# A decoder layer in split fp32: the first stage begins with another order of loads and norm weights, and three plain feature tiles instead of two

## The chip, the cores and the metric

The kernel runs on one core of one Trainium2 chip. Five engines work side by side, each through its own queue in order: TensorE (PE; its weight loads are shown apart as PEld), VectorE (DVE), ScalarE (ACT), GpSimd (POOL) and SyncE (SP, which here only issues DMAs). They meet through semaphores. The metric is the device time of one execution in microseconds. The kernel before took 1367.01 us (median of three runs, 1365.49 to 1369.76).

## What is computed

One decoder layer on 512 tokens of width 1024, in fp32. Every sub-layer stands between an RMSNorm before and one after. Only the first lines matter for the change:

```python
def rmsnorm(x, w):
    y = xf * lax.rsqrt(jnp.mean(xf * xf, axis=-1, keepdims=True) + EPS)
    return (y * w.astype(jnp.float32)).astype(x.dtype)
def swiglu(x, w_gu, w_down):                     # w_gu: 1024 x 5632, w_down: 2816 x 1024
    g, u = jnp.split(x @ w_gu, 2, axis=-1)
    return (jax.nn.silu(g) * u) @ w_down
h = h + 0.5 * rmsnorm(swiglu(rmsnorm(h, ffn1_pre_w), ffn1_w_gu, ffn1_w_down), ffn1_post_w)
h = h + rmsnorm(token_mixing(rmsnorm(h, mix_pre_w), ...), mix_post_w)
h = h + 0.5 * rmsnorm(swiglu(rmsnorm(h, ffn2_pre_w), ffn2_w_gu, ffn2_w_down), ffn2_post_w)
```

The token mixing (a gated linear recurrence, a dilated attention and a memory attention, gated and projected) lies in the middle and is not edited.

## The kernel before

**Number form.** Every fp32 operand is split into a rounded part (`hi`, made by ACT, line 161) and the rest (`lo`, made by DVE, line 158). A product is three matmuls in the fast fp32r form: hi with hi, hi with lo, lo with hi (`mm3`, lines 341 to 343). Tiles are called `xhi`/`xlo` for the normed, transposed input, `w` for both halves of a weight tile, `st` for a weight tile as loaded (a ring of 4, 512 KB each), `s` for general slots, `ps` and `px` for PSUM banks (5 and 3).

**Two ways to make a feature tile.** A feature tile is 128 columns of the gate weights with the 128 matching columns of the up weights, over all 512 tokens. In the plain way (`gu_plain`, line 444) it takes 2 weight columns x 8 slices of the inner dimension x 3 passes x 2 token halves = 96 matmuls of 256 columns. In the other way (`gu` and `pair`, lines 435 and 366) the two columns are one 2x2 block product made of 7 smaller products, 7 x 4 x 3 = 84 matmuls of 256 columns (`product`, lines 361 to 363). That way needs sums of weight blocks (`sum` tiles, a ring of 5; two per tile are made by DMAs that POOL issues and that add `sh` or `st` onto a loaded block, line 303) and sums of input blocks (`t1` to `t4`), which exist only when all four token tiles are normed.

**The opening.** Of the 22 feature tiles of the first stage, the first two (`PLAN`, line 49) are plain, so that TensorE can begin with the first 256 tokens. `first` (line 1022) loads the token tiles 0 and 1 (two halves of 256 KB each) and the norm weights, spread to all 128 partitions by two DMAs of 256 KB (`bcast_gain`, line 164). Each token tile then goes through `normed` (line 184): two squares with a running sum on ACT (line 174), the variance on DVE (line 180), the power -1/2 on POOL (line 181), two products with the norm weights on DVE (line 190), eight transposes on TensorE (line 352). `prenorm` splits the result (`split`, line 160) and keeps a raw copy for the block sums (line 208). In this part `strict` is set: DMAs, ACT's and DVE's main instructions keep the order of the program. Later a list scheduler orders each engine by estimated times, and `spawn`, `tick` and `need` decide when a task's next piece is written.

**After it** come 20 feature tiles in the 7-product way, in chunks of 2, 4, 4, 4, 4, 4 features; the down projections of a chunk stand between the feature tiles of the next. Then the mixing and a second feed-forward stage of the same form, which starts from token tiles that come out of the stage before it.

Of the kernel before, what the change touches and what calls it, by code (L numbers as in the profile page):

```python
# [17 lines left out]
P = 128  # L18
# [28 lines left out]
LAT = dict(comb=1.0, mem0=0.5, mem1=8.0, mem2=1.5, hg=1.5, hgx=6.0, hg1=6.0, hg2=11.0, hg3=6.0, hg4=6.0, dil0=4.0, dil1=17.0, dil2=5.0,  # L47
           dil3=3.0, norm=8.0, mnorm=5.0, mload=10.0, start=0.1, step=2.0, keep=2.0)
PLAN = dict(early1=2, plain1=2, early2=2, plain2=2)
HALVES = (slice(0, 512), slice(512, 1024))  # L50


class Layer:
# [3 lines left out]
    def __init__(self, ctx, tc):  # L57
# [30 lines left out]

        self.strict = False


# [72 lines left out]
    def bcast_gain(self, w):  # L164
# [4 lines left out]
        return g  # L169

    def square(self, src, hf, step):

        s = self.small.tile([P, 1], F32, tag=f"ss{hf}", bufs=8, name=f"ss{hf}_{self.uid()}")
        self.pin(self.nc.scalar.activation(self.slot(src.shape), src, AF.Square, scale=1.0 / (32.0 * step), accum_out=s))
        return s
# [7 lines left out]

    def normed(self, src, gain, lat, bank):

        r = self.rstd([self.square(src[hf], hf, 1.0) for hf in range(2)], 1.0)
        us = []
        for hf in range(2):
            u = self.slot()
            self.pin(self.nc.vector.scalar_tensor_tensor(out=u, in0=src[hf], scalar=r, in1=gain[hf], op0=ALU.mult, op1=ALU.mult))  # L190
            us.append(u)
        yield lat
        for hf, u in enumerate(us):
            pt = bank((P, 4, P))
            for k in range(4):
                self.transpose(pt[:, k, :], u[:, k * P:(k + 1) * P])
            yield pt

    def prenorm(self, src, gain, t, lat, raw):
# [6 lines left out]
        def keep(hf):  # L206
            raw[t, hf] = self.slot((P, 4, P))
            nc.scalar.copy(raw[t, hf], pts[hf])

        wait = self.strict and t < 2  # L210
        for x in self.normed(src, gain, lat, self.psum if self.strict and t == 1 else self.paux):
            if isinstance(x, float):
                yield x
                continue
            hf = len(pts)
            pts.append(x)
            self.split(self.xhi[hf][:, :, ts], self.xlo[hf][:, :, ts], x)
            if not wait and (t < 2 or hf == 0):
                keep(hf)
        if wait:  # L220
            def later():
                yield LAT['keep']
                keep(0)
                keep(1)
            self.spawn(later())
        if t < 2:
# [32 lines left out]
    def wsplit(self, src, slot=False):  # L259
        hi, lo = self.unit(src.shape, slot), self.unit(src.shape, slot)  # L260
        self.split(hi, lo, src)
        return hi, lo

    def wcol(self, st, slot=False):

        ws = [self.wsplit(st[:, 4 * i:4 * i + 4, :], slot) for i in range(2)]
        return [(ws[k // 4][0][:, k % 4, :], ws[k // 4][1][:, k % 4, :]) for k in range(KD)]

# [16 lines left out]
    def wops(self, w, c1, c2, by_load):  # L285
# [34 lines left out]

        def get(j):
            if j not in ops:
                if j == 6:
# [97 lines left out]
    def ffn(self, w_gu, w_down, w_post, ready, reload, after, chunks, early, plain):  # L421
# [21 lines left out]

        def gu_plain(w, act, cs):
            n = cs.stop - cs.start
            pg, pu = self.psum((P, n)), self.psum((P, n))
            self.proj_T(pg, w[0], self.uT, cs)
            self.proj_T(pu, w[1], self.uT, cs)
            sg = self.slot((P, n))
            nc.scalar.activation(sg, pg, AF.Silu)  # L450
            self.tt(sg, sg, pu, ALU.mult)
            self.split(act[0][:, cs], act[1][:, cs], sg)
# [16 lines left out]

        tasks, heads = [ready[0]()], []  # L470
        for i in range(early):
            heads.append([[next(gw), next(uw)], new_act()])
            if i == 0:
                tasks.append(ready[1]())
        for i in range(early):
            for j in range(2):
                if i == 0:
                    self.need(tasks[0][j])
                heads[i][0][j] = self.wcol(heads[i][0][j], i >= 2)
        self.strict = False  # L480
        for i in range(2):
            self.need(*tasks[i])
            for w, act in heads:
                gu_plain(w, act, slice(i * HT, (i + 1) * HT))
        f0, before, ws = 0, None, []
# [522 lines left out]
def layer_kernel(ctx, tc, a, nbias, hmask, out):  # L1008
# [12 lines left out]

    def first():
        hs = [load_x(t) for t in range(2)]
        gpre.extend(L.bcast_gain(a["ffn1_pre_w"][0]))
        return [L.spawn(L.prenorm(hs[t], gpre, t, 0.0, raw)) for t in range(2)]

    def second():
        def task(h, t):
            yield LAT['start']
            yield from L.prenorm(h, gpre, t, LAT['step'], raw)  # L1030
        return [L.spawn(task(load_x(t), t)) for t in range(2, NT)]
# [33 lines left out]
    def store(h, t):  # L1065
        for c, n in ((0, 512), (512, 256), (768, 256)) if t == NT - 1 else ((0, 512), (512, 512)):
# [4 lines left out]
    ready = L.ffn(a["ffn1_w_gu"][0], a["ffn1_w_down"][0], a["ffn1_post_w"][0], [first, second],  # L1071
                  reload(lambda t, hf: x[t * P:(t + 1) * P, HALVES[hf]]), follow(h1, a["mix_pre_w"][0]), CHUNKS1, PLAN['early1'], PLAN['plain1'])
    z = L.mixing(a, ready, nbias)
    ready = L.out_proj(z, a["w_out"][0], a["mix_post_w"][0], reload(lambda t, hf: h1[t][hf]), follow(h2, a["ffn2_pre_w"][0]))
# [43 lines left out]
```

## Time and profile before

| | |
|---|---|
| median of three runs | 1367.01 us |
| the profiled execution | 1367.62 us |
| its span, first to last instruction | 1365.8 us |
| PE busy | 1331.6 us, 97% of the span |
| DVE, ACT, POOL busy | 1050.7, 742.2, 107.0 us |
| moved by DMA | 185.76 MB, mean 136 GB/s |

The span is 1.8 us shorter than the execution that it belongs to. Busy times of a pipelined engine overlap a little, so the distance from one matmul's start to the next says more than its duration. A wait is shown as the idle time in front of an instruction and what ended it; the engine with the longest wait is not always the one that sets the end.

### The profile page before, as it was taken

To read this page: it belongs to the slowest core of one execution; us is meant where nothing else is said; L and a number is where in the kernel's file an instruction comes from. 1 tells how busy PE (TensorE), PEld (TensorE's weight loads), DVE (VectorE), ACT (ScalarE), POOL (GpSimd) and SP (SyncE) were. 2 spreads that over 40 slices of the span, in tenths; PEclk is the share of its full clock that TensorE was granted. 3 is DMA by queue.
4 is the path that set the end of the run, shared out by engine and by line. 5 is a ranking of instruction groups with operands and counts; after the bars stand their busy time and mean duration, and the time that the engine had idled before them with its cause. 6 is when DMAs were issued, how large, how long until landed. Compare 5 with 4: busy or idle time off the path is not lost.

```text
span 1365.8 us, 24324 instructions
## 1 busy us (share of the span) xinstructions
PE 1331.6 (97%) x9197; PEld 1233.0 (90%) x9197; DVE 1050.7 (77%) x1996; ACT 742.2 (54%) x1527; POOL 107.0 (8%) x140
## 2 busy tenths in 40 slices
PE   6999999999999999999999999999999999999997
PEld 6999999999789888899899999999889999999996
DVE  6887776777798975598888988897478877677765
ACT  6665544555467655355554755566366655445541
POOL 1111111110100000000000100000011111111100
PEclk9999999999999999999999999999999999999999
DMA  9676565554435335334224333335465765655513
GB/s 271 141 182 184 148 156 142 143 151 125 168 94 177 96 98 163 123 102 117 63 78 124 100 95 93 108 94 154 135 190 135 186 181 151 152 139 148 146 47 139
DMA packets 238123, 185.76 MB, mean 136 GB/s; under 512 B 9109, under 2 KB 198966, under 8 KB 238006
## 3 DMA queue, kind: packets, MB, share of 16 engines
q1 hardware_dynamic: 224246, 160.02, 39.5%
q0 software_dynamic: 12032, 21.04, 9.4%
q10 hardware_dynamic: 1728, 3.15, 0.6%
q8 instruction: 72, 1.18, 0.3%
q14 instruction: 45, 0.37, 0.1%
HBM read 153.73 MB, written 9.47 MB: 119 GB/s over the span
## 4 chain that ended last, share of the span: by engine, by line
PE 87%; DVE 6%; issue 3%; DMA 2%; ACT 1%; POOL 1%; SPq 0%; POOLq 0%; DVEq 0%; ACTq 0%
PE ps L361 17%; PE ps L363 17%; PE ps L362 17%; PE ps L341 6%; PE ps L342 6%; PE ps L343 6%; PE px L341 5%; PE px L342 5%; PE px L343 5%; PE px L348 4%; DVE s L158 2%; PE px L352 1%; DVE w L158 1%; POOL r L181 1%; DVE s L244 1%
## 5 line engine op out<-in xcount | busy, mean ns | idle before, releaser
L161 ACT ACTIVATE w<-sum 128x512 fp32r<-128x512 f32 x288 | 180.2, 631 | 215.9 <-PE ps L362 180.3
L158 DVE TENSOR_TENSOR w<-sum,w 128x512 fp32r<-128x512 f32 x288 | 196.9, 687 | 76.9 <-ACT w L161 75.9
L361 PE MATMUL ps<-xhi,w 128*128 128x256 f32 x864 | 246.3, 285 | 0.9 <-ACT s L379 0.9
L363 PE MATMUL ps<-xhi,w 128*128 128x256 f32 x864 | 244.8, 283 | 0.0
L362 PE MATMUL ps<-xlo,w 128*128 128x256 f32 x864 | 244.4, 283 | 0.0
L161 ACT ACTIVATE w<-st 128x512 fp32r<-128x512 f32 x260 | 162.9, 630 | 126.7 <-PE ps L362 90.0
L158 DVE TENSOR_TENSOR w<-st,w 128x512 fp32r<-128x512 f32 x260 | 177.2, 688 | 39.3 <-ACT w L161 37.9
L158 DVE TENSOR_TENSOR s<-s,s 128x256 f32<-128x256 f32 (+3 forms) x316 | 176.8, 564 | 16.2 <-ACT s L161 4.6
L361 PEld LDWEIGHTS ps<-xhi,w 128*128 128x128 f32 x864 | 165.6, 192 | 3.8 <-ACT s L379 1.2
L362 PEld LDWEIGHTS ps<-xlo,w 128*128 128x128 f32 x864 | 165.6, 192 | 2.4 <-issue 0.2
L363 PEld LDWEIGHTS ps<-xhi,w 128*128 128x128 f32 x864 | 165.5, 192 | 0.0
L158 DVE TENSOR_TENSOR sum<-sum,st 128x512 f32<-128x512 f32 x176 | 120.4, 687 | 10.9 <-issue 5.0
L158 DVE TENSOR_TENSOR s<-s,ps 128x256 f32<-128x256 f32 (+1 forms) x194 | 92.3, 476 | 29.4 <-PE ps L343 24.0
L341 PE MATMUL px<-s,s 128*128 128x512 f32 x288 | 112.6, 391 | 0.0
L342 PE MATMUL px<-s,s 128*128 128x512 f32 x288 | 112.5, 391 | 0.0
L343 PE MATMUL px<-s,s 128*128 128x512 f32 x288 | 112.0, 389 | 0.0
L361 PE MATMUL ps<-t4hi,w 128*128 128x256 f32 x288 | 81.9, 284 | 0.8 <-ACT s L382 0.8
L361 PE MATMUL ps<-t3hi,w 128*128 128x256 f32 x288 | 82.6, 287 | 0.0
L362 PE MATMUL ps<-t3lo,w 128*128 128x256 f32 x288 | 82.0, 285 | 0.0
L361 PE MATMUL ps<-t1hi,w 128*128 128x256 f32 x288 | 81.7, 284 | 0.0
L363 PE MATMUL ps<-t1hi,w 128*128 128x256 f32 x288 | 81.6, 283 | 0.0
L362 PE MATMUL ps<-t2lo,w 128*128 128x256 f32 x288 | 81.5, 283 | 0.0
(186 smaller groups left out, 3344.2 us busy)
## 6 DMA issues: line engine op xcount, KB each, us to landing
st<-in_ffn_w_gu_dram SPq DMA_DIRECT2D x48, 512.0 KB, 4.9
st<-in_w_in_dram SPq DMA_DIRECT2D x48, 512.0 KB, 3.7
st<-in_ffn_w_down_dram SPq DMA_DIRECT2D x44, 512.0 KB, 3.8
sum<-in_ffn_w_gu_dram SPq DMA_DIRECT2D x80, 256.0 KB, 3.4
sh<-in_ffn_w_gu_dram SPq DMA_DIRECT2D x40, 256.0 KB, 3.8
sum<-sh POOLq DMA_DIRECT2D x40, 256.0 KB, 3.6
sum<-st POOLq DMA_DIRECT2D x40, 256.0 KB, 3.3
sum<-in_w_in_dram SPq DMA_DIRECT2D x32, 256.0 KB, 2.9
```

The source lines that it names most:

```text
L158: self.pin(self.nc.vector.tensor_tensor(out=out, in0=a, in1=b, op=op))
L161: self.pin(self.nc.scalar.activation(hi, src, AF.Copy))
L181: self.nc.gpsimd.tensor_tensor(out=r, in0=v, in1=self.mhalf[:, :1], op=ALU.pow)
L244: self.nc.vector.scalar_tensor_tensor(out=h[hf][:, cs], in0=y[hf][:, cs], scalar=r, in1=h[hf][:, cs], op0=ALU.mult, op1=ALU.add)
L341: mm(out, lhsT=lhs[0], rhs=rhs[0], start=first, stop=False)
L342: mm(out, lhsT=lhs[0], rhs=rhs[1], start=False, stop=False)
L343: mm(out, lhsT=lhs[1], rhs=rhs[0], start=False, stop=last)
L348: self.nc.tensor.matmul(out, lhsT=lhsT, rhs=rhs, start=start, stop=stop, **k)
L352: self.nc.tensor.transpose(out, in_, self.ident)
L361: mm(out, lhsT=lh, rhs=rh, start=first and k == 0, stop=False, skip_group_check=True)
L362: mm(out, lhsT=lh, rhs=rl, start=False, stop=False, skip_group_check=True)
L363: mm(out, lhsT=ll, rhs=rh, start=False, stop=k == 3, skip_group_check=True)
```

## The change

The first stage's opening is written anew. The norm weights come as two rows of 2 KB on ACT's DMA queue; TensorE multiplies a column of ones with each (after four products of the ones with a row of the identity matrix), and the spread weights are read from PSUM by DVE, later copied to SBUF by ACT (`spread_gain`). The big loads are issued in another order. The two normed halves of a token tile are written one by one, so that instructions of the two token tiles interleave (`fine`). The hi parts of the first weights are made between the two token tiles (`whigh`), the lo parts after all input lo parts (`wlow`). The first plain tile is multiplied pass by pass over gate and up columns, hi with hi first (`by_pass`). `PLAN['early1']` and `PLAN['plain1']` go from 2 to 3. Operands of the 7-product tiles in the first stage are placed behind the last split of the input (`behind`).

```diff
-           dil3=3.0, norm=8.0, mnorm=5.0, mload=10.0, start=0.1, step=2.0, keep=2.0)
-PLAN = dict(early1=2, plain1=2, early2=2, plain2=2)
+           dil3=3.0, norm=8.0, mnorm=5.0, mload=10.0, start=100.0, step=2.0, keep=0.5)
+PLAN = dict(early1=3, plain1=3, early2=2, plain2=2)
...
+    def spread_gain(self, w):
+        nc = self.nc
+        ones = self.slot((1, P))
+        self.pin(nc.vector.memset(ones, 1.0))
+        g = []
+        for hf in range(2):
+            row = self.slot((1, 512))
+            self.pin(nc.scalar.dma_start(out=row, in_=w[HALVES[hf]].unsqueeze(0)))
+            g.append(row)
+        out = []
+        for row in [self.ident[0:1, :]] * 4 + g:
+            ps = self.psum((P, row.shape[-1]))
+            nc.tensor.matmul(ps, lhsT=ones, rhs=row, start=True, stop=True)
+            out.append(ps)
+        return out[4:]
...
-    def normed(self, src, gain, lat, bank):
+    def normed(self, src, gain, lat, bank, fine=False):
         r = self.rstd([self.square(src[hf], hf, 1.0) for hf in range(2)], 1.0)
         us = []
+        if fine:
+            yield 0.0
         for hf in range(2):
+            if fine and hf:
+                yield 0.0
             u = self.slot()
...
-            nc.scalar.copy(raw[t, hf], pts[hf])
+            self.pin(nc.scalar.copy(raw[t, hf], pts[hf]))
         wait = self.strict and t < 2
-        for x in self.normed(src, gain, lat, self.psum if self.strict and t == 1 else self.paux):
+        banks = iter((self.paux, self.psum) if self.strict and t == 1 else (self.paux, self.paux))
+        for x in self.normed(src, gain, lat, lambda shape: next(banks)(shape), self.strict and t < 2):
             if isinstance(x, float):
                 yield x
                 continue
             hf = len(pts)
             pts.append(x)
             self.split(self.xhi[hf][:, :, ts], self.xlo[hf][:, :, ts], x)
+            if self.first and t == NT - 1 and hf == 1:
+                self.behind = [next(i for i in reversed(nc.cur_bb.bb.instructions) if i.engine == e.engine) for e in (nc.vector, nc.scalar)]
...
-            self.spawn(later())
+            self.keeps.append(self.spawn(later()))
...
+    def whigh(self, st, slot=False):
+        out = []
+        for i in range(2):
+            src = st[:, 4 * i:4 * i + 4, :]
+            hi, lo = self.unit(src.shape, slot), self.unit(src.shape, slot)
+            self.pin(self.nc.scalar.activation(hi, src, AF.Copy))
+            out.append((hi, lo, src))
+        return out
+    def wlow(self, ws):
+        for hi, lo, src in ws:
+            self.tt(lo, src, hi.bitcast(F32), ALU.subtract)
+        return [(ws[k // 4][0][:, k % 4, :], ws[k // 4][1][:, k % 4, :]) for k in range(KD)]
     def wcol(self, st, slot=False):
-
-        ws = [self.wsplit(st[:, 4 * i:4 * i + 4, :], slot) for i in range(2)]
-        return [(ws[k // 4][0][:, k % 4, :], ws[k // 4][1][:, k % 4, :]) for k in range(KD)]
+        return self.wlow(self.whigh(st, slot))
...
         def get(j):
+            with ExitStack() as order:
+                for ins in self.behind:
+                    order.enter_context(self.tc.issue_after(ins))
+                return make(j)
+        def make(j):
...
-        def gu_plain(w, act, cs):
+        def gu_plain(w, act, cs, by_pass=False):
             n = cs.stop - cs.start
             pg, pu = self.psum((P, n)), self.psum((P, n))
-            self.proj_T(pg, w[0], self.uT, cs)
-            self.proj_T(pu, w[1], self.uT, cs)
+            if by_pass:
+                for i, j in ((0, 0), (0, 1), (1, 0)):
+                    for ps, ww in ((pg, w[0]), (pu, w[1])):
+                        for k in range(KD):
+                            nc.tensor.matmul(ps, lhsT=ww[k][i], rhs=self.uT[k][j][:, cs], start=i + j + k == 0,
+                                             stop=i == 1 and k == KD - 1)
+                            self.tick(0.2158 * n / T)
+            else:
+                self.proj_T(pg, w[0], self.uT, cs)
+                self.proj_T(pu, w[1], self.uT, cs)
...
         tasks, heads = [ready[0]()], []
+        order = [(i, j) for i in range(early) for j in range(2)]
         for i in range(early):
-            heads.append([[next(gw), next(uw)], new_act()])
-            if i == 0:
+            heads.append([[None, None], new_act()])
+        for n, (i, j) in enumerate(order):
+            if n == 3:
                 tasks.append(ready[1]())
-        for i in range(early):
-            for j in range(2):
-                if i == 0:
-                    self.need(tasks[0][j])
-                heads[i][0][j] = self.wcol(heads[i][0][j], i >= 2)
+            heads[i][0][j] = next((gw, uw)[j])
+        if self.first:
+            self.need(tasks[0][0])
+            high = self.whigh(heads[0][0][0])
+            self.need(tasks[0][1])
+        for n, (i, j) in enumerate(order):
+            if n < 2 and not self.first:
+                self.need(tasks[0][j])
+            if n == 4:
+                self.need(*self.keeps)
+            if n == 3 and self.first:
+                for task in tasks[1]:
+                    self.advance(task)
+            heads[i][0][j] = self.wlow(high) if self.first and n == 0 else self.wcol(heads[i][0][j], i >= 2)
         self.strict = False
         for i in range(2):
             self.need(*tasks[i])
-            for w, act in heads:
-                gu_plain(w, act, slice(i * HT, (i + 1) * HT))
+            for n, (w, act) in enumerate(heads):
+                gu_plain(w, act, slice(i * HT, (i + 1) * HT), self.first and i == 0 and n == 0)
...
+        gpre.extend(L.spread_gain(a["ffn1_pre_w"][0]))
         hs = [load_x(t) for t in range(2)]
-        gpre.extend(L.bcast_gain(a["ffn1_pre_w"][0]))
-        return [L.spawn(L.prenorm(hs[t], gpre, t, 0.0, raw)) for t in range(2)]
+        t0 = L.spawn(L.prenorm(hs[0], gpre, 0, 0.0, raw))
+        L.advance(t0)
+        t1 = L.spawn(L.prenorm(hs[1], gpre, 1, 0.0, raw))
+        for t in (t0, t1, t1):
+            L.advance(t)
+        return [t0, t1]
     def second():
         def task(h, t):
             yield LAT['start']
+            if t == 2:
+                for hf in range(2):
+                    g = L.slot()
+                    L.pin(nc.scalar.copy(g, gpre[hf]))
+                    gpre[hf] = g
```

Line numbers in the rows of the changed kernel are its own: there line 160 is DVE's subtraction, 163 and 298 ACT's rounding, 187 the spreading, 200 the variance, 215 the product with the norm weights, 389 to 391 the three passes, 400 the transpose, 499 the product pass by pass.

SP's queue, from the last half of token tile 1 on. Before (`s_132`, `s_133` are the norm weights, `st_164` and `st_166` the first gate and up weights, `s_170` to `s_175` token tiles 2 and 3):

```order
L141 DMA s_129<-in_x_dram 128x512
L141 DMA s_132<-in_ffn_pre_w_dram 128x512
L141 DMA s_133<-in_ffn_pre_w_dram 128x512
L141 DMA st_164<-in_ffn_w_gu_dram 128x8x128
L141 DMA st_166<-in_ffn_w_gu_dram 128x8x128
L141 DMA s_170<-in_x_dram 128x512
L141 DMA s_171<-in_x_dram 128x512
L141 DMA s_174<-in_x_dram 128x512
L141 DMA s_175<-in_x_dram 128x512
L141 DMA st_178<-in_ffn_w_gu_dram 128x8x128
L141 DMA st_180<-in_ffn_w_gu_dram 128x8x128
```

In the changed kernel (`st_184`, `st_186`, `st_188`: gate 0, up 0, gate 1; `st_198` up 1; `st_200`, `st_202` the third tile; `s_190` to `s_195` token tiles 2 and 3):

```order
L143 DMA s_147<-in_x_dram 128x512
L143 DMA st_184<-in_ffn_w_gu_dram 128x8x128
L143 DMA st_186<-in_ffn_w_gu_dram 128x8x128
L143 DMA st_188<-in_ffn_w_gu_dram 128x8x128
L143 DMA s_190<-in_x_dram 128x512
L143 DMA s_191<-in_x_dram 128x512
L143 DMA s_194<-in_x_dram 128x512
L143 DMA s_195<-in_x_dram 128x512
L143 DMA st_198<-in_ffn_w_gu_dram 128x8x128
L143 DMA st_200<-in_ffn_w_gu_dram 128x8x128
L143 DMA st_202<-in_ffn_w_gu_dram 128x8x128
```

The norm weights are gone from this queue, gate 1 stands ahead of the token tiles 2 and 3, and two loads for the third tile follow up 1.

DVE's first instructions. Before (`v` the variance, `r` the power of it from POOL, `s_146` to `s_162` the normed halves of token tiles 0 and 1):

```order
L180 TENSOR_SCALAR v_142<-ss_15_136,ss_17_139 128x1
L190 SCALAR_TENSOR_TENSOR s_146<-s_124,r_143,s_132 128x512
L190 SCALAR_TENSOR_TENSOR s_148<-s_125,r_143,s_133 128x512
L180 TENSOR_SCALAR v_156<-ss_23_150,ss_25_153 128x1
L190 SCALAR_TENSOR_TENSOR s_160<-s_128,r_157,s_132 128x512
L190 SCALAR_TENSOR_TENSOR s_162<-s_129,r_157,s_133 128x512
L158 TENSOR_TENSOR xlo_90<-px_184,xhi_88 128x4x128
L158 TENSOR_TENSOR xlo_91<-px_191,xhi_89 128x4x128
L158 TENSOR_TENSOR w_199<-st_164,w_198 128x512
L158 TENSOR_TENSOR w_203<-st_164,w_202 128x512
L158 TENSOR_TENSOR xlo_90<-ps_206,xhi_88 128x4x128
L158 TENSOR_TENSOR xlo_91<-ps_213,xhi_89 128x4x128
```

In the changed kernel (`ps_138`, `ps_140` hold the spread norm weights; `s_160`, `s_172` token tile 0, `s_174`, `s_176` token tile 1):

```order
L200 TENSOR_SCALAR v_156<-ss_22_150,ss_24_153 128x1
L215 SCALAR_TENSOR_TENSOR s_160<-s_142,r_157,ps_138 128x512
L200 TENSOR_SCALAR v_168<-ss_29_162,ss_31_165 128x1
L215 SCALAR_TENSOR_TENSOR s_172<-s_143,r_157,ps_140 128x512
L215 SCALAR_TENSOR_TENSOR s_174<-s_146,r_169,ps_138 128x512
L215 SCALAR_TENSOR_TENSOR s_176<-s_147,r_169,ps_140 128x512
L160 TENSOR_TENSOR xlo_90<-px_204,xhi_88 128x4x128
L160 TENSOR_TENSOR xlo_91<-px_211,xhi_89 128x4x128
L160 TENSOR_TENSOR xlo_90<-px_224,xhi_88 128x4x128
L160 TENSOR_TENSOR xlo_91<-ps_231,xhi_89 128x4x128
L160 TENSOR_TENSOR w_219<-st_184,w_218 128x512
L160 TENSOR_TENSOR w_222<-st_184,w_221 128x512
```

The second half of token tile 0 now stands behind the variance of token tile 1, and all four input lo parts stand ahead of the first weight lo parts.

TensorE's first instructions. Before (four groups of four transposes, then the three passes slice by slice):

```order
L352 MATMUL px_184<-ident,s_146 128x128 x4
L352 MATMUL px_191<-ident,s_148 128x128 x4
L352 MATMUL ps_206<-ident,s_160 128x128 x4
L352 MATMUL ps_213<-ident,s_162 128x128 x4
L341 MATMUL ps_244<-xhi_88,w_198 128x256
L342 MATMUL ps_244<-xlo_90,w_198 128x256
L343 MATMUL ps_244<-xhi_88,w_199 128x256
```

In the changed kernel (`ps_320` gate 0, `ps_321` up 0, `s_124` the ones; two of the four products with the identity are left off):

```order
L187 MATMUL ps_134<-ident,s_124 128x128
L187 MATMUL ps_136<-ident,s_124 128x128
L187 MATMUL ps_138<-s_126,s_124 128x512
L187 MATMUL ps_140<-s_128,s_124 128x512
L400 MATMUL px_204<-ident,s_160 128x128 x4
L400 MATMUL px_211<-ident,s_172 128x128 x4
L400 MATMUL px_224<-ident,s_174 128x128 x4
L400 MATMUL ps_231<-ident,s_176 128x128 x4
L499 MATMUL ps_320<-xhi_88,w_218 128x256 x4
L499 MATMUL ps_320<-xhi_89,w_221 128x256 x4
L499 MATMUL ps_320<-xlo_90,w_218 128x256 x4
L499 MATMUL ps_320<-xlo_91,w_221 128x256 x4
```

In front of the transposes stand the products with the ones. The first plain tile then starts with groups of four that run hi with hi, and the lo of the input comes second; the lo of the weights (`w_219`, `w_222`) stands behind these rows.

## Rows read from the trace of the kernel before

**Rows 1.** The page, sections 1 and 4: busy time by engine; the chain's shares

```profile
span 1365.8 us, 24324 instructions
PE 1331.6 (97%) x9197; PEld 1233.0 (90%) x9197; DVE 1050.7 (77%) x1996; ACT 742.2 (54%) x1527; POOL 107.0 (8%) x140
...
PE 87%; DVE 6%; issue 3%; DMA 2%; ACT 1%; POOL 1%; SPq 0%; POOLq 0%; DVEq 0%; ACTq 0%
```

**Rows 2.** Timeline, PE: start, duration, engine, line, tiles, idle before

```profile
9.53 2.32 PE L352 MATMUL px<-ident,s 128*128 128x128 f32 x8 [9.53 <-DVE s L190]
12.28 1.97 PE L352 MATMUL ps<-ident,s 128*128 128x128 f32 x8 [0.43 <-DVE s L190]
14.08 0.58 PE L341 MATMUL ps<-xhi,w 128*128 128x256 f32 x1
15.94 0.58 PE L342 MATMUL ps<-xlo,w 128*128 128x256 f32 x1 [1.28 <-DVE xlo L158]
...
16.54 0.41 PE L341 MATMUL ps<-xhi,w 128*128 128x256 f32 x1
...
21.02 0.39 PE L341 MATMUL ps<-xhi,w 128*128 128x256 f32 x1
...
22.04 0.28 PE L342 MATMUL ps<-xlo,w 128*128 128x256 f32 x1
...
25.03 0.28 PE L343 MATMUL ps<-xhi,w 128*128 128x256 f32 x1
...
43.31 0.28 PE L361 MATMUL ps<-xhi,w 128*128 128x256 f32 x1
```

**Rows 3.** Timeline, DVE, 8 to 13 us

```profile
8.73 0.75 DVE L190 SCALAR_TENSOR_TENSOR s<-s,r,s 128x512 f32<-128x512 f32 x1 [3.48 <-DMA s<-in_ffn_pre_w_dram]
...
10.60 0.21 DVE L180 TENSOR_SCALAR v<-ss,ss 128x1 f32<-128x1 f32 x1
...
11.47 1.42 DVE L190 SCALAR_TENSOR_TENSOR s<-s,r,s 128x512 f32<-128x512 f32 x2 [0.67 <-POOL r L181]
```

**Rows 4.** Stretches of 10 us: busy us (instructions) by engine, PEclk, DMA share, GB/s

```profile
0.00:10.00 10.00, 0.47 (x2) 0.47 (x3) 1.04 (x3) 4.04 (x9) 1.29 (x8) 1.00 0.74 224
10.00:20.00 10.00, 8.21 (x36) 6.88 (x35) 8.67 (x16) 7.78 (x17) 1.10 (x2) 1.00 1.06 316
```

**Rows 5.** Timeline, ACT, 6 to 14 us

```profile
6.83 0.63 ACT L174 ACTIVATE s<-s 128x512 f32<-128x512 f32 x1
...
7.36 0.19 ACT L174 ACTIVATION_READ_ACCUMULATOR s<-s 128x1 f32 x1
...
12.38 1.14 ACT L161 ACTIVATE w<-st 128x512 fp32r<-128x512 f32 x2
...
13.43 0.60 ACT L161 ACTIVATE xhi<-ps 128x512 fp32r<-128x512 f32 x1
```

**Rows 6.** Line 867, DMAs that ACT issues

```profile
DMA to landing us min/median/max: 2.0/2.0/2.7
```

**Rows 7.** Timeline, PE at 796 us: 16 fp32 products of 128 columns, two records each

```profile
795.94 3.81 PE L348 MATMUL px<-s,s 128*128 128x128 f32 x32
```

**Rows 8.** Timeline, 48 to 67 us: DVE, ACT and PE

```profile
48.13 0.68 DVE L158 TENSOR_TENSOR w<-sh,w 128x512 fp32r<-128x512 f32 x1
...
61.13 0.69 DVE L158 TENSOR_TENSOR sum<-sum,st 128x512 f32<-128x512 f32 x1 [4.95 <-issue]
...
61.85 1.67 ACT L161 ACTIVATE w<-sum 128x512 fp32r<-128x512 f32 x3 [3.71 <-DVE sum L158]
...
64.35 0.39 PE L361 MATMUL ps<-xhi,w 128*128 128x256 f32 x1 [0.86 <-ACT s L379]
...
66.82 0.39 PE L361 MATMUL ps<-t4hi,w 128*128 128x256 f32 x1 [0.77 <-ACT s L382]
```

**Rows 9.** The chain of waits, 0 to 80 us: start, us, what

```profile
48.84 5.04 DMA sh<-in_ffn_w_gu_dram
```

**Rows 10.** Tile st, 0 to 30 us: loads of 512 KB

```profile
DMA to landing us min/median/max: 5.0/8.0/10.8
```

More of the change, by code (lines that the diff above doesn't have):

```diff
@@ L89, in __init__ @@
         self.strict = False
+        self.first, self.behind, self.keeps = True, [], []
     def spawn(self, gen):
@@ L1072, in layer_kernel @@
                   reload(lambda t, hf: x[t * P:(t + 1) * P, HALVES[hf]]), follow(h1, a["mix_pre_w"][0]), CHUNKS1, PLAN['early1'], PLAN['plain1'])
+    L.first, L.behind = False, []
     z = L.mixing(a, ready, nbias)
```

## The prediction

> **What bounds the kernel now.** I read the page first. PE is busy for 1331.6 of 1365.8 us, and 87% of the chain that ended last is PE [rows 1]. So the kernel ends when PE's queue is through, and an edit counts only where PE is idle, where it runs at its lower clock, or where it gets more or fewer matmuls. PE's timeline shows the first of these places: the opening. Transposes start at 9.53, the first main matmul at 14.08, and then PE stands for 1.28 us until an `xlo` is there; the second main matmul starts at 15.94 and from there the queue hardly stops [rows 2]. The same view shows the clock. [...] The clock thus rose about 5.3 us after 15.94. Everything later runs at 0.12 us, and a second place with a wait that the change can reach is at 64.35 and 66.82, where PE waits 0.86 and 0.77 us for ACT [rows 8].
>
> What ends last inside the opening: DVE waits 3.48 us for the norm weights and can make its first product only at 8.73 [rows 3], though the squares of token tile 1 run at 6.83 on ACT [rows 5]. The norm weights stand behind the whole of token tiles 0 and 1 on SP's queue.
>
> **The new opening, step by step.** The two rows of norm weights are issued by ACT at the start. The DMAs that ACT issues land 2.0 to 2.7 us after issue [rows 6], so I put them in at about 3.2. A fp32 product takes two records, 3.81 / 32 = 0.119 us each for 128 columns at the full clock [rows 7], 0.238 at the lower one. The four products with the identity are 4 x 2 x 0.238 = 1.9 us (about 1.4 to 3.3), each spread half of 512 columns 2 x 4 x 0.238 = 1.9 us. The halves of the weights are therefore ready at about 5.2 and 7.1. Token tile 1 is the later input: its last square starts at 6.83 and is read at 7.36 to 7.55 [rows 5], its variance follows at 7.6, and the product with the weights started 0.87 us after the variance (10.60 to 11.47 [rows 3]). DVE's order sets the second product of token tile 0 between the two, at 7.75, and the two of token tile 1 after it, 0.7 apart (1.42 / 2 [rows 3]), at 8.47 and 9.15. A group of four transposes starts 0.80 after its product does (8.73 to 9.53 [rows 2, 3]) and takes 1.97 / 2 = 1.0 [rows 2]: 8.55, 9.55 and 10.55.
>
> ACT makes the second `xhi` of token tile 0 1.15 after its first transpose (12.28 to 13.43 [rows 2, 5]), at 9.7; two weight halves follow, 1.05 for both (12.38 to 13.43 [rows 5]), and then the first `xhi` of token tile 1: 9.7 + 0.6 + 1.05 = 11.35. The first matmul came 0.65 after the start of its `xhi` (13.43 to 14.08 [rows 2, 5]): 12.0. The second follows 0.21 later at 12.2, since hi with hi comes first and asks for no `xlo`. Before it was at 15.94: **-3.73 us**. DVE's part fits beneath: four `xlo` and two weight lo at 0.69 each [rows 8] from 10.3, the last pair of `xlo` from 11.95, lie ahead of PE's passes that use them. Gate 0's bytes are not late: ahead of its end stand 1.05 MB of tokens and 0.52 MB of weights, 1.57 MB, against 224 GB/s x 10 us = 2.24 MB moved by 10.0 [rows 4].
>
> **The clock.** In the old opening only 16 transposes came ahead of the first main matmul, and those main matmuls still ran at 0.213 [rows 2]. In the new one six ordinary products keep PE busy from 1.4 to 7.1 without a break, 5.7 us, against the 5.3 us of matmuls after which the clock rose [rows 2]. I expect that it rises at the end of the spreading and lasts until 12.0. Then the first 25 matmuls take 0.120 instead of 0.213: 25 x 0.093 = **-2.3 us**. What could undo it is the stretch from 7.1 to 12.0 with nothing on PE but the 16 transposes; no row shows the clock falling or lasting across such a stretch, so the term's bounds are 0 and -2.3, and the range keeps both.
>
> [...]
>
> **The third plain tile.** It takes 96 matmuls in place of 84: 12 x 0.120 = **+1.44 us**, a price with no cover, since PE is the bound. Its up weights (`st_202`) go into the buffer of up 0, which is free after DVE's sixth subtraction from 11.95, at 11.95 + 6 x 0.69 = 16.1. Loads landed 8.0 us after issue in the median, 10.8 at most [rows 10]: 24.1. On ACT its two roundings, two `xhi` and the raw copy of `px_341` follow, 5 x 0.6 = 3.0, and the transpose into `px_374`, which waits for that copy, can go at 27.1. PE has 108 matmuls and 12 transposes ahead of it: 12.0 + 108 x 0.120 + 12 x 0.123 (half of 1.97 / 8 [rows 2]) = 26.5. So PE stands for **+0.6 us** there, between 0 (5.0 us landing) and 3.4 (10.8). At the lower clock PE would come 2.3 later and not wait at all.
>
> **The wait at 64 us.** DVE's `w<-sh` at 48.13 came 4.8 us after the first 7-product matmul (43.31), only then could the next `sh` load (48.84, 5.04 us [rows 9]) go, the POOL-issued add behind it and DVE's `sum` at 61.13, for which ACT waited 3.71 with what PE needed queued behind it [rows 2, 8]. In the changed kernel the first 7-product matmul comes at 43.31 - 3.73 - 2.3 + 0.6 + 96 x 0.120 = 49.4, while the loads and block sums don't wait for the third tile. They get 6 us of lead against 1.63 us (0.86 + 0.77) of stall: **-1.63 us**. The bounds are -1.63 and 0. The placing behind the last input split and the copies of the norm weights to SBUF (2 x 0.6 on ACT) lie under PE's plain tiles. The second stage's opening is reordered a little by the scheduler; I cost it at 0 +- 0.5.
>
> **Sum.** -3.73 - 2.3 + 1.44 + 0.6 - 1.63 = -5.6 us. The profiled execution took 1367.62, so 1362.0; the median of the runs is 0.6 lower, so **1361.4**. From 0.3% on (4.1 us, so below 1362.9 or above 1371.1) a difference can be told from none.
>
> **The rivals.**
> 1. The clock is low again at 12.0, or never rises in front. For it: the stretch with transposes only. Against: the 5.7 us of products. -3.73 + 1.44 - 1.63 = -3.9: 1363.1.
> 2. The wait at 64 us moves along with the 7-product tiles. For it: DVE and ACT make more splits in between and the `sum` tiles are still five. Against: 6 us of lead. 1361.4 + 1.63 = 1363.0.
> 3. The opening does not do what it says: the rows land as late as the norm weights did (DVE free at 8.73, so about 6.4 before the spreading) and the second half is ready at 6.4 + 2 x 1.9 = 10.2, where 7.1 was planned; `s_172` was to start at 7.75, so all behind it is 2.5 later: 1361.4 + 2.5 = 1363.9; without the clock 1365.6. Against: 2.0 to 2.7 us on ACT's queue [rows 6].
> 4. Slower: `st_202` lands late behind the loads for the 7-product tiles, and ACT, in order, holds `xhi` and the raw copy behind its rounding, so PE stops at `px_374`. Each us of landing beyond 10.4 - 3.0 = 7.4 after the issue is a us lost; the gain of 6.2 without the stall is eaten at 7.4 + 6.2 = 13.6 us after the issue. At 20 us, twice the longest but one kind of load seen (10.8 [rows 10]), it costs 12.6: 1373.4. Against: no load here took over 10.8, which gives 1364.2.
>
> **Chances.** Forecast 0.46; rival 1 0.26; rival 2 0.13; rival 3 0.09; rival 4 0.06. Of the forecast's 0.46, 0.42 lie below 1362.9; rivals 1 and 2 lie on that bound, and I give 0.14 of their 0.39 to its lower side; rival 3 is within 0.3%; of rival 4 0.02 lie above 1371.1. So faster 0.56, same 0.42, slower 0.02. The forecast's own range is 1360.0 to 1363.0. The range asked for reaches down to 1359.6 (the opening half a us better, no stall, the second stage 0.5 better) and up to 1365.6 (rival 3 without the clock).
>
> **What would show it.** In the changed profile: the second main matmul near 12.2; matmuls after it 0.12 apart and not 0.21; the spread halves ended by 7.1; at PE's last transposes for token tile 3 (about 26.5) a wait under a us; no wait over 0.3 in the first two 7-product tiles; 96 matmuls of the third plain tile. The forecast is wrong by mechanism if the first matmuls are 0.21 apart, if they begin after 13.5, or if PE waits over 2 us between 20 and 50.

## The result, and the profile after

The changed kernel took 1373.56 us (median of six runs, 1372.46 to 1375.13), the kernel before 1368.15 (median of six, 1365.49 to 1369.76): ratio 1.0041, interval 1.0029 to 1.0053. It is slower by 5.4 us where 5.6 us less were forecast, and lies outside the range. The profiled execution took 1373.13 us, its span 1371.3 against 1365.8. From the page, in the form of [rows 1]:

```profile
span 1371.3 us, 24352 instructions
PE 1342.4 (98%) x9221; PEld 1241.5 (91%) x9221; DVE 1048.2 (76%) x1989; ACT 741.4 (54%) x1524; POOL 105.6 (8%) x138
```

PE is still the bound, with 24 more records: 12 matmuls of the third plain tile and 12 of the spreading (the columns are those of [rows 1]). PE's timeline of the opening, which answers to [rows 2]:

```profile
1.36 2.07 PE L187 MATMUL ps<-ident,s 1*128 1x128 f32 x8 [1.36 <-POOL ident masks.py:199]
3.23 3.62 PE L187 MATMUL ps<-s,s 1*128 1x512 f32 x4
7.39 1.12 PE L400 MATMUL px<-ident,s 128*128 128x128 f32 x4 [0.54 <-DVE s L215]
9.86 1.97 PE L400 MATMUL px<-ident,s 128*128 128x128 f32 x8 [1.35 <-DVE s L215]
11.62 1.06 PE L400 MATMUL ps<-ident,s 128*128 128x128 f32 x4
13.18 2.07 PE L499 MATMUL ps<-xhi,w 128*128 128x256 f32 x8 [0.51 <-ACT xhi L163]
15.05 1.91 PE L499 MATMUL ps<-xlo,w 128*128 128x256 f32 x8
16.76 2.70 PE L499 MATMUL ps<-xhi,w 128*128 128x256 f32 x13
19.30 1.12 PE L499 MATMUL ps<-xlo,w 128*128 128x256 f32 x8
...
30.07 0.60 PE L400 MATMUL px<-ident,s 128*128 128x128 f32 x4
...
31.82 0.28 PE L391 MATMUL ps<-xhi,s 128*128 128x256 f32 x1
36.16 0.58 PE L389 MATMUL ps<-xhi,s 128*128 128x256 f32 x1 [4.06 <-ACT s L506]
36.54 0.42 PE L390 MATMUL ps<-xlo,s 128*128 128x256 f32 x1
...
39.11 0.41 PE L390 MATMUL ps<-xlo,s 128*128 128x256 f32 x1
```

The opening did what was worked out until 7.1: the spreading ends at 6.85. Then the last group of transposes for token tile 1 comes later than forecast (11.62 for 10.55), the first matmul at 13.18 instead of 12.0. From 15.05 to 16.76 the 8 matmuls are 1.71 / 8 = 0.21 us apart and take 1.91 us; the 8 from 19.30 on take 1.12 and are 0.95 / 8 = 0.12 apart. The kernel before has the same two distances, 4.48 / 21 = 0.213 us from 16.54 to 21.02 and 2.99 / 25 = 0.120 from 22.04 to 25.03 [rows 2]. The column PEclk, the granted share of the full clock, reads 1.00 from 10 to 20 in both kernels, so in the opening the clock is my reading of the distances: by them it rose near 19, not ahead of 12. And at 36.16 stands a wait that the forecast doesn't have: 4.06 us for ACT's line 506, a SiLU. Behind it 12 distances from 36.54 to 39.11 are 0.214 us: the clock had fallen to its lower level, and some 16 matmuls cost 16 x 0.094 = 1.5 us more. Here the column PEclk shows it too, 0.66 (columns as in [rows 4]):

```profile
35.00:40.00 5.00, 3.84 (x20) 3.84 (x21) 4.49 (x8) 2.94 (x6) 0.31 (x1) 0.66 0.69 127
```

ACT's timeline shows what stood ahead of that SiLU:

```profile
30.71 0.60 ACT L163 ACTIVATE xhi<-px 128x512 fp32r<-128x512 f32 x1 [2.29 <-PE px L400]
...
33.78 0.63 ACT L163 ACTIVATE t1hi<-s 128x512 fp32r<-128x512 f32 x1
34.43 1.28 ACT L506 ACT_TABLE_LOAD   x1
35.73 0.38 ACT L506 ACTIVATE s<-ps 128x256 f32<-128x256 f32 x1
```

This SiLU reads the first gate column's bank (a bank is here one `ps` buffer), whose 24 matmuls were over by about 21. Plain products take banks in turn from five (`ps`), one for each 24 matmuls, so the sixth group, the up half of the third tile, needs the bank that this SiLU frees. ACT's queue has it behind the last `xhi` of token tile 3, which waits for the transposes at 30.07, and behind six more roundings and copies and a table load. In the kernel before the same SiLU ran just in time: it was at 33.64, and by count (120 matmuls and 16 transposes from the first matmul on) PE came to its sixth group at about 34.4.

```profile
33.64 0.38 ACT L450 ACTIVATE s<-ps 128x256 f32<-128x256 f32 x1
```

The two waits of [rows 8] at the first 7-product tiles are gone, as forecast. Two of the same kind now stand in the second stage, where the kernel before has none; and PE's clock fell once more there, behind a wait of 1.99 us (PEclk 0.72; in the kernel before 1.92 us at that place, and PEclk 1.00 from 1006 to 1011). First the kernel before, then the changed one:

```profile
1008.33 0.39 PE L342 MATMUL ps<-xlo,w 128*128 128x256 f32 x1 [1.92 <-DVE xlo L158]
1018.81 0.63 PE L352 MATMUL px<-ident,s 128*128 128x128 f32 x4 [0.83 <-DVE s L190]
```

```profile
1011.31 0.39 PE L390 MATMUL ps<-xlo,w 128*128 128x256 f32 x1 [1.99 <-DVE xlo L160]
1022.69 0.63 PE L400 MATMUL px<-ident,s 128*128 128x128 f32 x4 [0.34 <-DVE s L215]
1059.06 0.39 PE L409 MATMUL ps<-xhi,w 128*128 128x256 f32 x1 [0.65 <-ACT s L427]
1061.52 0.39 PE L409 MATMUL ps<-t4hi,w 128*128 128x256 f32 x1 [0.78 <-ACT s L430]
```

```profile
1010.00:1015.00 5.00, 3.69 (x21) 3.69 (x21) 4.56 (x9) 4.98 (x12) 0.86 (x1) 0.72 0.61 208
```

How the 5.5 us of the span add up: the same transposes of the mixing start at 359.84 before and at 362.54 after, +2.70. From the opening's parts: -2.4 (second matmul at about 13.5 for 15.94), +1.44 (third tile), +4.06 and +1.5 (wait and clock), -1.63: +3.0. At the second stage's first wait it is still +2.98 (1011.31 for 1008.33), at the transposes behind it +3.88 (1022.69 for 1018.81), though the wait there is 0.49 shorter: 3.88 + 0.49 - 2.98 = 1.4 for the clock. With 0.65 + 0.78 of new waits it is +5.3, within 0.2 of the span.

### The profile page after: what moved, and what is told of

Its sections match the earlier page's. It is cut to its first block, busy times and chain, and to the rows that moved or that the text cites. A ratio compares the mean times of both kernels' runs of the same rounds, so it can differ in the third digit from the quotient of the medians.

```text
span 1371.3 us, 24352 instructions
## 1 busy us (share of the span) xinstructions
PE 1342.4 (98%) x9221; PEld 1241.5 (91%) x9221; DVE 1048.2 (76%) x1989; ACT 741.4 (54%) x1524; POOL 105.6 (8%) x138
## 4 chain that ended last, share of the span: by engine, by line
PE 86%; DVE 5%; issue 3%; DMA 3%; ACT 2%; POOL 1%; SPq 0%; POOLq 0%; DVEq 0%; ACTq 0%
PE ps L409 16%; PE ps L411 16%; PE ps L410 16%; PE ps L389 6%; PE ps L391 5%; PE ps L390 5%; PE px L389 5%; PE px L390 5%; PE px L391 5%; PE px L396 4%; PE px L400 1%; DVE s L160 1%; POOL r L201 1%; DVE s L272 1%; DVE w L160 1%
## 5 line engine op out<-in xcount | busy, mean ns | idle before, releaser
L409 PE MATMUL ps<-xhi,w 128*128 128x256 f32 x852 | 242.8, 285 | 0.7 <-ACT s L427 0.7
L411 PE MATMUL ps<-xhi,w 128*128 128x256 f32 x852 | 241.4, 283 | 0.0
L410 PE MATMUL ps<-xlo,w 128*128 128x256 f32 x852 | 241.0, 283 | 0.0
L163 ACT ACTIVATE w<-st 128x512 fp32r<-128x512 f32 x234 | 146.8, 631 | 129.3 <-PE ps L410 92.0
L409 PEld LDWEIGHTS ps<-xhi,w 128*128 128x128 f32 x852 | 163.3, 192 | 3.4 <-ACT s L427 0.9
L411 PEld LDWEIGHTS ps<-xhi,w 128*128 128x128 f32 x852 | 163.2, 192 | 0.0
L411 PE MATMUL ps<-t2hi,w 128*128 128x256 f32 x284 | 80.4, 283 | 0.0
```

Of the source, the lines that this page charges most:

```text
L163: self.pin(self.nc.scalar.activation(hi, src, AF.Copy))
L409: mm(out, lhsT=lh, rhs=rh, start=first and k == 0, stop=False, skip_group_check=True)
L410: mm(out, lhsT=lh, rhs=rl, start=False, stop=False, skip_group_check=True)
L411: mm(out, lhsT=ll, rhs=rh, start=False, stop=k == 3, skip_group_check=True)
```

## The experiments

**Two plain tiles in the new opening (e1).**

```diff
-PLAN = dict(early1=3, plain1=3, early2=2, plain2=2)
+PLAN = dict(early1=2, plain1=2, early2=2, plain2=2)
```

> The new opening with two plain tiles as before. Theory B (a PSUM bank): the sixth group of 24 plain matmuls needs the bank that the SiLU of the first group frees, and that SiLU stands in ACT's queue behind the splits of token tiles 2 and 3, whatever the number of plain tiles. [...] The wait at the first 7-product tiles (1.6) may come back. 4.06 - 1.7 + 1.45 + 1.44 = 5.2 less than the changed kernel, 3.6 less with that wait: 1368.3 to 1370. Theory L (the third tile's weights are late and hold ACT): no wait at the sixth group, 1366 to 1368.

1368.15 us, ratio 1.0003 (0.9992 to 1.0015). PE waits:

```profile
28.72 0.39 PE L390 MATMUL ps<-xlo,w 128*128 128x256 f32 x1 [0.90 <-DVE xlo L160]
31.68 0.39 PE L389 MATMUL ps<-xhi,w 128*128 128x256 f32 x1 [1.38 <-ACT s L506]
63.07 0.39 PE L409 MATMUL ps<-xhi,w 128*128 128x256 f32 x1 [0.98 <-ACT s L427]
65.53 0.39 PE L409 MATMUL ps<-t4hi,w 128*128 128x256 f32 x1 [0.76 <-ACT s L430]
```

The SiLU's wait is still there with two tiles, as theory B said, and 2.7 us shorter; the waits of [rows 8] are back. The sum of the expectation has 1.7 for the wait that stays, an estimate, and 1.45 for a clock that keeps its level behind it, which no run shows: behind the measured 1.38 us the clock fell (PEclk 0.83 from 30 to 40, 14 distances of 0.213 us from 32.08 to 35.06). A wait of 0.90 stands shortly ahead, at 28.72. Theory L, no wait, falls for this kernel.

**Three plain tiles in the old opening (e2).** The same line of the kernel before, with 3 for 2.

> The old opening with three plain tiles. Theory B: PE starts 2.5 us later than in the changed kernel and asks for the sixth bank at about 34.5, ACT's SiLU (33.64 before) moves back by the third tile's weight roundings to about 36: a wait of 1 to 2.5 us at the sixth group, and 1.44 for the extra matmuls; the wait at 64 us (1.63) gone: 1368.2 + 1.4 + 1.7 - 1.6 = 1369.7, 1368.5 to 1371. Rival (the new order of loads and products itself causes the stall): no wait at the sixth group, 1368.0.

1377.81 us, ratio 1.0073 (1.0058 to 1.0088): 8 us worse than expected.

```profile
29.87 0.65 PE L352 MATMUL px<-ident,s 128*128 128x128 f32 x4 [2.21 <-ACT s L208]
31.78 1.09 PE L352 MATMUL px<-ident,s 128*128 128x128 f32 x4 [1.26 <-ACT s L208]
43.92 0.58 PE L341 MATMUL ps<-xhi,s 128*128 128x256 f32 x1 [3.77 <-ACT s L450]
```

The wait for the SiLU came, 3.77, without the new opening. In the old order the third tile's late weights hurt as well, as theory L would have it: ACT waits 1.72 us for a weight load (at 27.01) and PE 2.21 and 1.26 for the raw copies behind it, and the clock fell twice (PEclk 0.68 from 30 to 35, 0.61 from 45 to 50). By the ratios the third tile costs 10 us in the old opening and 5 in the new one (1.0041 against e1's 1.0003), each with some 2 us of noise.

**The first SiLU ahead of the splits of token tiles 2 and 3 (e3).** The transposes of these two token tiles are written later, and the splits of the input and of its block sums `t1` to `t3` are placed behind the SiLU (the lines left out do it for the block sums and note the SiLU):

```diff
-           dil3=3.0, norm=8.0, mnorm=5.0, mload=10.0, start=100.0, step=2.0, keep=0.5)
+           dil3=3.0, norm=8.0, mnorm=5.0, mload=10.0, start=100.0, step=6.0, keep=0.5)
...
-            self.split(self.xhi[hf][:, :, ts], self.xlo[hf][:, :, ts], x)
+            with ExitStack() as order:
+                if self.first and self.silu is not None:
+                    order.enter_context(self.tc.issue_after(self.silu))
+                self.split(self.xhi[hf][:, :, ts], self.xlo[hf][:, :, ts], x)
...
+        if self.first:
+            yield 6.0
         self.tt(t1, x11, x12, ALU.subtract)
...
```

> The changed kernel with the transposes and splits of token tiles 2 and 3 written later, so that the first SiLU stands ahead of them on ACT. Theory B: the SiLU runs by about 27, the bank is free when PE asks at about 32, the wait of 4.06 goes and the fall of the clock behind it (1.45) too: 1373.6 - 5.5 = 1368.1, 1367 to 1369.5. Theory L or a rival by which ACT's and DVE's work is simply too much for these 20 us: a wait of 3 us or more stays between 30 and 50 us at another operand, 1371 or more.

1366.09 us, ratio 0.9988 (0.9978 to 0.9999); by the ratios 0.53%, 7.2 us (some 2 either way), less than the changed kernel. ACT's SiLU, and the stretch in which the wait was:

```profile
24.34 0.38 ACT L514 ACTIVATE s<-ps 128x256 f32<-128x256 f32 x1
```

```profile
30.00:40.00 10.00, 10.00 (x85) 10.00 (x85) 8.92 (x16) 6.39 (x13) 1.74 (x2) 1.00 0.78 186
```

PE is busy throughout at PEclk 1.00. With theory B's wait go 5.5 us, 4.06 and the clock's 1.5, within the noise of the 7.2. (In the two profiles 1.1 more is the landing of token tile 1: the last square at 7.04, not 8.18.) The rival, too much work for ACT and DVE, falls. In the mixing this kernel is 5.0 us ahead of the kernel before (the same transposes at 354.89), yet its end is only 1.4 ahead (1364.4 for 1365.8); e6 asks why.

**All 128 rows in the spreading (e4).** On top of e3:

```diff
-        ones = self.slot((1, P))
+        ones = self.slot((P, P))
...
-            row = self.slot((1, 512))
-            self.pin(nc.scalar.dma_start(out=row, in_=w[HALVES[hf]].unsqueeze(0)))
+            row = self.slot((P, 512))
+            self.pin(nc.vector.memset(row, 0.0))
+            self.pin(nc.scalar.dma_start(out=row[0:1, :], in_=w[HALVES[hf]].unsqueeze(0)))
...
-        for row in [self.ident[0:1, :]] * 4 + g:
+        for row in [self.ident] * 4 + g:
```

> As e3, and the six products that spread the norm weights use all 128 rows (ones of 128 x 128, the weights' row in a tile of zeros, the whole identity), at the same count of products and columns. Theory R (products of one row do not lift the clock): first main matmuls 0.12 and not 0.21 apart, 27 x 0.093 = 2.5 us less than e3 if the bank is free: 1365.6. Theory G (the clock falls again in the stretch that holds only transposes): first main matmuls 0.21 apart until about 19 as in e3, same time as e3 within 0.5.

1366.05 us, ratio 0.9989 (0.9979 to 0.9999).

```profile
1.36 2.08 PE L188 MATMUL ps<-ident,s 128*128 128x128 f32 x8 [1.36 <-POOL ident masks.py:199]
4.28 3.75 PE L188 MATMUL ps<-s,s 128*128 128x512 f32 x4 [0.84 <-DMA s<-in_ffn_pre_w_dram]
7.82 2.36 PE L409 MATMUL px<-ident,s 128*128 128x128 f32 x12
10.28 0.63 PE L409 MATMUL ps<-ident,s 128*128 128x128 f32 x4
11.74 1.23 PE L508 MATMUL ps<-xhi,w 128*128 128x256 f32 x8 [0.84 <-ACT xhi L163]
12.80 1.12 PE L508 MATMUL ps<-xlo,w 128*128 128x256 f32 x8
...
50.26 0.50 PE L399 MATMUL px<-s,s 128*128 128x512 f32 x1 [1.51 <-DVE s L160]
```

The same places of e3's PE, and what ended e4's wait at 50.26 on DVE:

```profile
10.49 1.06 PE L408 MATMUL ps<-ident,s 128*128 128x128 f32 x4
...
13.93 1.91 PE L507 MATMUL ps<-xlo,w 128*128 128x256 f32 x8
15.63 1.81 PE L507 MATMUL ps<-xhi,w 128*128 128x256 f32 x13
```

```profile
49.52 0.68 DVE L160 TENSOR_TENSOR s<-st,s 128x512 fp32r<-128x512 f32 x1
```

Theory R holds for the clock: from 12.80 on the 8 matmuls take 1.12 us and are 0.12 apart, in e3 1.91 and 0.21, until about 16. e7 and e8, which spread with 128 rows too, start in the same way (8 matmuls in 1.12 us from 12.83 and 13.06). Theory G, that the clock falls over the stretch of transposes, is refuted for this stretch: the last four transposes already take 0.63 us, in e3 1.06, and the clock is still up at 11.74. It did not rise at the end of the spreading, though: the first four transposes are still 0.21 apart, the rise came near 8.6, behind the spreading's end at 8.03. For the time, theory R's 1365.6 and theory G's "as e3" both fit. PE's lead was taken back in part at 50.26: PE waited for the lo part of a down projection's weights, which stands on DVE behind work for the 7-product tiles.

**SiLU's table loaded at the start (e5).** The changed kernel and one line behind the issue of the two rows:

```diff
+        self.pin(nc.scalar.activation(self.slot((1, P)), ones, AF.Silu))
```

> The changed kernel with one tiny SiLU at the start, so that ACT loads the table there and not in front of the first real SiLU. Theory B (PE waits for that SiLU's bank): the SiLU comes 1.28 us earlier, the wait of 4.06 shrinks to about 2.8, and the clock may keep its level: 1373.6 - 1.3 = 1372.3, or 1370.8 if the clock does not fall. Theory L (late weights of the third tile, or DVE): the table is not what ends the wait, 1373.6.

1369.68 us, ratio 1.0025 (1.0015 to 1.0035).

```profile
32.66 0.39 PE L390 MATMUL ps<-xhi,s 128*128 128x256 f32 x1 [2.64 <-ACT s L507]
```

2.64 us for the 2.8 expected: ACT's chain up to the SiLU is the wait, by its size too. From the last `xhi` to the SiLU ACT took 3.62 us (28.63 to 32.25), in the changed kernel 5.02, so the figure does not hang on the landing, which was earlier here (first matmul at 11.41). By the ratios the time fell by 0.16%, 2.2 us; the noise of some 2 us does not tell theory B's 1.3 from its 2.8. In the profile the clock still fell behind the wait (PEclk 0.80 from 35 to 40).

**POOL's additions behind the last power (e6).** On top of e3:

```diff
-        self.nc.gpsimd.tensor_tensor(out=r, in0=v, in1=self.mhalf[:, :1], op=ALU.pow)
+        self.power = self.nc.gpsimd.tensor_tensor(out=r, in0=v, in1=self.mhalf[:, :1], op=ALU.pow).ins
...
-                self.nc.gpsimd.dma_start(out=u, in_=x, accum_op=ALU.add)
+                with self.tc.issue_after(self.power):
+                    self.nc.gpsimd.dma_start(out=u, in_=x, accum_op=ALU.add)
```

> e3 with POOL's adding DMAs placed behind the last power of the token tiles. Theory P: in e3 the lead of 5.5 us over the kernel before was lost at the start of the second stage because POOL waited 2.76 us for a weight load with the last token tile's power queued behind it; PE then waited 2.48 instead of 0.83 and its clock fell (1.5). Without that: 1366.1 - 1.7 - 1.5 = 1363.0. Rival D: the sums come later and the wait moves to the first 7-product tiles of the second stage: 1366.

1364.16 us, ratio 0.9980 (0.9969 to 0.9991): faster than the kernel before. In e3 POOL and PE showed

```profile
1012.31 0.86 POOL L353 DMA_DIRECT2D sum<-st  x1 [2.76 <-DMA st<-in_ffn_w_gu_dram]
1012.87 0.89 POOL L201 TENSOR_TENSOR r<-v,mhalf 128x1 f32<-128x1 f32 x1
```

```profile
1014.69 0.63 PE L408 MATMUL px<-ident,s 128*128 128x128 f32 x4 [2.48 <-DVE s L215]
```

and here POOL's powers are all done before the first addition, at 1013.25; PE's waits are

```profile
1014.24 0.63 PE L409 MATMUL px<-ident,s 128*128 128x128 f32 x4 [1.48 <-DVE s L215]
1019.29 0.39 PE L398 MATMUL ps<-xhi,w 128*128 128x256 f32 x1 [0.78 <-ACT s L515]
```

with PEclk 1.00 from 1000 to 1020. The wait shrank by 1.0, not 1.65, and the clock stayed. The rival, that it moves to the first 7-product tiles, is not seen: PE has no wait between 1020 and 1070, where e3 has 0.31 and 0.78. A new one of 0.78 stands at 1019.29, for a SiLU again (line 515). That the time fell against e3 (0.9988) is not shown: the two intervals overlap.

**All of it, with three and with two plain tiles (e7, e8).** e6 with the edits of e4 and e5, and PLAN at 3 or 2.

> e6 with the full-row spreading of e4 and the early table of e5, three plain tiles. If PE sets the end in the opening: e6 less 2.3 (clock), 1360.7. Rival V (DVE's splits set the pace between 20 and 50 us, so that a lead of PE in the opening is taken back at about 50 us as in e4, where PE waited 1.51): within 0.7 of e6.

> As e7 with two plain tiles. The third tile costs 1.44 of PE and 8 splits' time of ACT and DVE less or more: if the third tile buys the 1.63 at the first 7-product tiles, as I predicted, e8 is equal to e7 within 0.5; if DVE sets the pace there, two plain tiles leave it less time ahead of the 7-product tiles and e8 is slower than e7 by 1 to 3.

1365.45 us (0.9985, 0.9976 to 0.9995) and 1363.64 (0.9980, 0.9970 to 0.9990). With the clock up from the start e7 is no faster than e6, by the medians 1.3 us slower: the 2.3 are not there. That speaks for rival V, whose 0.7 holds by the ratios alone; PE waits 1.25 us at 49.97 for DVE, as in e4. With two tiles DVE is indeed short of time, PE waits 0.97, 0.53 and 0.93 between 39 and 43 us, 2.43 in all, and still e8 is not slower than e7 (by the medians 1.8 us faster, by the ratios 0.7, where equal or slower was expected): the 1.44 of 12 matmuls and e7's 1.25 are gone, 2.69. Which of e6, e7, e8 is best these runs do not tell; all three beat both kernels.

**The changed kernel once more (e9).**

> The changed kernel once more, for a second profile. Theory B: the last square of token tile 1 may start anywhere from 6.1 to 8.2 (as in the profiles with this order of loads), but the wait at the sixth group of matmuls comes again and ends with the first SiLU at 34 to 36, the longer the earlier PE began: 3.5 to 6 us, with a fall of the clock behind it. Rival (the late landing of the one profile made it slow): with an earlier landing no wait over 2 us there.

```profile
35.47 0.58 PE L389 MATMUL ps<-xhi,s 128*128 128x256 f32 x1 [4.45 <-ACT s L506]
```

1376.13 us, one run; the last square of token tile 1 at 7.94, the wait 4.45, PEclk 0.70 from 30 to 40. The wait is the kernel's, not one run's. In this run e3's wait on POOL is there as well:

```profile
1021.10 0.86 POOL L345 DMA_DIRECT2D sum<-st  x1 [2.72 <-DMA st<-in_ffn_w_gu_dram]
```

```profile
1023.47 0.82 PE L400 MATMUL px<-ident,s 128*128 128x128 f32 x4 [2.43 <-DVE s L215]
```

In the first profile PE waited only 0.34 at that place, and its clock had fallen behind the 1.99 us ahead of it; here the same wait of 1.99 left the clock up, and it fell behind the 2.43. So the second stage lost its time in different ways from run to run.

## Why the prediction was wrong

- **The step that failed** is the third tile's "PE stands for +0.6 us there". I followed one chain through ACT, to the raw copy in front of `px_374`, and priced that; no wait stands there. I did not ask where the sixth group of products gets its bank: there are five, and ACT has the SiLU that frees the first one behind the splits. This one term was +4.06, and +1.5 for the clock behind it (e3, e5, e9). Two of the prediction's own signs came, a wait of over 2 us between 20 and 50 and first matmuls 0.21 apart.
- **Rival 4** had ACT's queue and the third tile right, and the releaser wrong: not a late load but ACT's own order. The 512 KB loads of the opening landed within 7.3 us, where its 1373.4 wanted one of 20; that this figure lies by the measured 1373.56 is luck.
- **The clock, -2.3**: did not come. I took 5.3 us of any products to be enough, which was my estimate from [rows 2]. Products of one row kept PE busy for 5.5 us and the main matmuls behind them were still 0.21 apart; behind the same count with 128 rows they were 0.12 apart (e4). The other doubt that I raised, a fall over the stretch of transposes, was the wrong one: in e4 the clock was up from about 8.6 to the first matmul at 11.74, with nothing but transposes and a wait between. In the kernel before, 16 transposes from 9.53 to 14.25 left the main matmuls behind them 0.213 apart [rows 2].
- **The opening, -3.73**: right mechanism, size -2.4. The 0.238 us for a record at the lower clock was an estimate, twice the 0.119 of [rows 7]; the first eight records, from 1.36 to 3.23, are 0.234 apart. I took the landing of token tile 1 from the profile before (last square at 6.83 [rows 5]). With the new order of loads this square starts between 6.11 and 8.18 in nine profiles; at 7.04 (e3) the first matmul came at 12.05, for 12.0 forecast.
- **The wait at 64 us, -1.63, and the third tile's +1.44**: right (e1 has the wait back).
- **The second stage, "0 +- 0.5"**: wrong, about +2.5 (5.5 less the 2.98 at its first wait). In the first profile it is the two new waits and the clock. No run was made to find the cause of the two waits; in e6 and e7, where POOL's additions stand behind the last power, they are gone, in e8 one of 0.60 is left. The reordering that the prediction priced at nothing put a second addition ahead of the last power, where the kernel before has one; in e3, e5 and e9 that addition waits for a load (2.76, 2.63 and 2.72 us) with the power behind it.

The misses add up: 1.3 (opening), 2.3 (clock), 5.0 (4.06 + 1.5 for 0.6) and 2.5 (second stage) are the 11.1 us between the 1362.0 forecast for the profiled execution and its 1373.13.

## What to carry to other kernels

When a product is added or starts earlier, follow the ring of PSUM banks: count the groups until a bank comes round again, and look up what stands ahead of its reader on that engine, table loads included (1.28 us here). Price a wait of TensorE with the slower matmuls that can stand behind it (1.5 us behind the 4.06 here). On an in-order engine a tiny operation behind one that waits for a transfer waits with it: 2.76 us for a power on POOL (e3), of which the better order gave TensorE 1.0 back (e6).

## What the runs showed that was not expected

- Behind 5.5 us of products with 1 row the first main matmuls were 0.21 apart, in six profiles of five kernels; behind about 6 us of the same with 128 rows they were 0.12 apart, in all three (e4, e7, e8).
- The clock fell behind waits of 4.06 and 1.99 us (the changed kernel), 2.48 (e3) and even 1.38 (e1), and did not behind 1.99 in e5 and e9, 1.92 in the kernel before or 1.51 in e6. At one place of the mixing it fell behind 1.79 us (383.81, the changed kernel, PEclk 0.66 from 384 to 389) and did not behind 1.78 (381.11, the kernel before, PEclk 1.00 from 381 to 386). What decides between them is open.
- Loads of the same order landed up to 2 us apart from run to run (last square 6.11 to 8.18).
